# Tokens and features on 512-byte addresses, the direct tiles moved behind three products, and two products exchanged

## The chip, the cores and the metric

The kernel runs on one core of one Trainium2 chip. The metric is device time in microseconds (us) of one execution. The kernel before took 2361.76 us, the median of three runs (2360.01 to 2362.44).

## The reference, cut to what matters

One layer of a streaming encoder over 2048 prompt tokens and 128 sample tokens (8 sequences of 16), model width 1024, float32 throughout:

```python
z = x @ w_in                       # 1024 -> 2824: q, k, v, output gate, 8 gate columns, attention q, k, v
hm = head_norm(mlstm(q, k, v, log gates)) * sigmoid(output gate)     # 4 heads x 128, in chunks
ha = sliding_window_attention(rope(qa), rope(ka), va, sinks)         # 8 query heads, 2 key heads
h = layer_norm(alpha * x + concat(hm, ha) @ w_out)
u = h @ w_up                       # 1024 -> 5632, value | gate
c = causal depthwise conv of width 3 over u
y = layer_norm(alpha * h + (silu(c_gate) * c_value) @ w_down)        # 2816 -> 1024
```

The outputs are y of both parts and the new states (mLSTM matrices, key and value rows, the last rows before the conv).

## The kernel before, in words

Every large product is made from float32 numbers split in two: `split` (lines 215 to 218) makes a high part by a cast to the type that TensorE takes (`scalar.copy`, ScalarE) and a low part by a subtraction (`vector.tensor_sub`, VectorE). A product is then three matmuls: high by high, high by low, low by high. One operand of a matmul is stationary (loaded into the array, 128 x 128), the other moves through it. The projections also use a seven-product scheme over 2 x 2 quadrants: products 1 to 7 take sums of quadrants of weights and of tokens.

There are four stages. The input projection (`i_dense`) runs over four token blocks (`IBLOCKS`); the sample tile, number 16, belongs to block 0. In a block it makes seven products for each of five groups `g` of 512 columns (`i_product`, L700), for block 0 also the sample tile's part (L710), and "direct" tiles (`i_direct`, L726): the remaining 264 columns (gates, key, value), one token tile at a time, without the seven-product scheme. Between them run small chains of the mLSTM and the attention. Then come the output projection (`group`, L222 to L224), the up projection (`f_product`, L1842) and the down projection (`f_downs`, L2045).

In groups 0 and 1 the weights are stationary and the tokens move; in groups 2 to 4 the tokens are stationary and the weights move. In the up projection the features move; in the output and down projection tokens or features are stationary.

The order of the matmuls is the order in which the program issues them. For the input projection it is the list `items`, made in `i_begin`: `("p", b, g, s)` is product s of group g in block b, `("t", b, i, e)` direct tile i of block b with the gate weights of edition e. `uq` lists the weight units in that order; `next_raw` issues a unit's load on SyncE's queue, `next_split` splits it, and `advance` does as many of both as there are free buffers (four raw slots `wraw`, eight halves). `x_load` loads token quadrants, `x_steps` makes their sums ("t1" to "t4") and splits, `x_single` those of the sample tile. VectorE and ScalarE take their work in an order that the framework chooses, SyncE's queue likewise.

At the start, block 0 has its direct tiles 2, 3 and 4 first, then products (g 0, s 1), (g 0, s 2), (g 1, s 1), (g 0, s 7), (g 0, s 6); its direct tiles 0 and 1 come at the end of the block, beside tiles 2 and 3 of block 1. Nine matmuls on zeros (`warm_up`, L325) stand ahead of all. Loads of the first quadrants are 512 KB each. After product (g 0, s 1) ScalarE copies its accumulator (bank A) to bank B (L775) before product 2 may go on in A.

Tiles lie in memory pools that are stacked by size, so a tile added to one pool moves all pools behind it. Before, the token halves (`oh`, `ol`) start 96 bytes past a multiple of 512 bytes in each partition, the features' halves 96 (products 2, 5, 3), 128 (product 4) or 480 bytes (products 1, 7, 6 and the down projection's `fu`) past one; the split weights lie at 192, 320, 448 and 64 past one, and two later slots (`wex`) at 96.

## Time and profile before

| what | value |
|---|---|
| median of the runs | 2361.76 us |
| time of the profiled execution | 2359.6 us |
| its span, first to last instruction | 2357.8 us |
| TensorE busy with matmuls | 2316.6 us, 98% of the span |
| VectorE busy | 1805.4 us, 77% |
| ScalarE busy | 1297.9 us, 55% |
| mean share of the DMA engines' time | 77.3% in the main queue |
| granted TensorE clock, mean | 0.997 |

PE is TensorE's matmul, PEld its weight load, which runs beside the matmul before it; DVE is VectorE, ACT ScalarE, POOL GpSimd, SPq the queue of transfers on SyncE. A matmul's recorded duration includes the time in the pipe, so matmuls overlap in the records; what a matmul costs is the busy time of a stretch divided by the number of matmuls in it. A `<-` names what a tile is made from, `x36` a count, and the bracket at the end of a row of the timeline the idle time before it and what ended that.

### The profile page before, as it was taken

The page shows a single profiled execution, that of the slowest core. Times are in us where ns is not written, and L with a number is a line of the kernel's source. Part 1 is how long each engine was busy: PE and PEld are TensorE (multiplying, and loading weights), DVE is VectorE, ACT ScalarE, POOL GpSimd, SP SyncE. Part 2 cuts the span into 40 slices and gives each one's busy share as a digit, 9 for nine tenths or more (in the row PEclk, how much of TensorE's full clock was granted, in tenths as well). Part 3 has the DMA queues.
Part 4 walks back from the last instruction along what each step waited for, and adds up shares of the span by engine and source line. Part 5 has one row for each costly group of instructions (what it writes and reads, how often), then busy time and mean ns, then how long its engine had stood idle before and what let it go on. Part 6 is the DMA issues. An engine that isn't in the chain of part 4 may idle for free.

```text
span 2357.8 us, 39882 instructions
## 1 busy us (share of the span) xinstructions
PE 2316.6 (98%) x14425; PEld 2123.4 (90%) x14425; DVE 1805.4 (77%) x3150; ACT 1297.9 (55%) x2465; POOL 243.4 (10%) x298
## 2 busy tenths in 40 slices
PE   8999999999999999999999999999999999999998
PEld 7999998999987777999999999999999978888876
DVE  8677586796678888987788677768766776795897
ACT  5353466676666664655556555555554544554643
POOL 0101101101212221300001000002100100000100
PEclk9999999999999999999999999999999999999999
DMA  7788899889977657787777989887988786757653
GB/s 278 263 308 291 282 290 313 285 289 319 301 259 247 210 208 251 264 324 277 281 270 252 309 314 318 303 271 263 321 286 265 230 283 203 240 186 226 233 181 108
DMA packets 296933, 624.98 MB, mean 265 GB/s; under 512 B 47004, under 2 KB 140192, under 8 KB 296736
## 3 DMA queue, kind: packets, MB, share of 16 engines
q1 hardware_dynamic: 295872, 619.29, 77.3%
q10 hardware_dynamic: 864, 3.15, 0.4%
q8 instruction: 114, 1.87, 0.3%
q14 instruction: 83, 0.68, 0.1%
HBM read 451.78 MB, written 170.56 MB: 264 GB/s over the span
## 4 chain that ended last, share of the span: by engine, by line
PE 73%; DVE 5%; DMA 2%; issue 2%; ACT 2%; POOL 0%; SPq 0%; DVEq 0%; ACTq 0%; POOLq 0%
PE dps L1842 18%; PE fup L1842 18%; PE dps L700 7%; PE dps L2045 7%; PE fht L2045 6%; PE fup L2045 6%; PE dps L222 2%; PE dps L224 2%; PE dps L223 2%; PE ppo L1337 1%; PE psc L1288 1%; PE ppt L1331 1%; PE dps L726 1%; DVE w L218 1%; DVE hl L218 1%
## 5 line engine op out<-in xcount | busy, mean ns | idle before, releaser
L1842 PE MATMUL dps<-hh,uw 128*128 128x384 f32 (+1 forms) x1848 | 481.0, 329 | 6.7 <-ACT u L1867 1.9
L1842 PE MATMUL fup<-hh,uw 128*128 128x384 f32 (+1 forms) x1848 | 479.8, 328 | 2.7 <-ACT u L1867 2.6
L1842 PEld LDWEIGHTS dps<-hh,uw 128*128 128x128 f32 x1848 | 330.0, 188 | 10.5 <-ACT u L1867 2.7
L1890 DVE SCALAR_TENSOR_TENSOR cc<-u,cw,cc 128x768 f32<-128x768 f32 (+1 forms) x264 | 252.4, 977 | 107.5 <-ACT cc L1888 105.5
L1842 PEld LDWEIGHTS fup<-hh,uw 128*128 128x128 f32 x1848 | 330.1, 188 | 4.0 <-ACT u L1867 3.5
L1842 PE MATMUL fup<-hl,uw 128*128 128x384 f32 (+1 forms) x924 | 302.8, 328 | 1.6 <-DVE hl L218 1.6
L1842 PE MATMUL dps<-hl,uw 128*128 128x384 f32 (+1 forms) x924 | 302.4, 327 | 0.0
L700 PE MATMUL dps<-w,oh 128*128 128x256 f32 x1344 | 259.3, 286 | 2.8 <-ACT zev L759 1.0
L218 DVE TENSOR_TENSOR w<-wraw,w 128x1024 fp32r<-128x1024 f32 (+2 forms) x167 | 190.4, 1148 | 58.8 <-ACT w L217 58.1
L217 ACT CAST w<-wraw 128x1024 fp32r<-128x1024 f32 (+2 forms) x167 | 163.0, 985 | 129.1 <-PE dps L700 52.9
L217 ACT CAST uw<-wraw 128x1024 fp32r<-128x1024 f32 x126 | 122.9, 978 | 189.3 <-PE dps L2045 108.8
L700 PEld LDWEIGHTS dps<-w,oh 128*128 128x128 f32 x1344 | 213.1, 189 | 14.7 <-issue 8.9
L1888 ACT ACTIVATE cc<-u,cw 128x768 f32<-128x768 f32 (+1 forms) x132 | 129.6, 998 | 123.0 <-DVE u L1881 61.4
L218 DVE TENSOR_TENSOR uw<-wraw,uw 128x1024 fp32r<-128x1024 f32 x126 | 142.4, 1132 | 71.0 <-ACT uw L217 70.2
L700 PE MATMUL dps<-w,ol 128*128 128x256 f32 x672 | 189.6, 282 | 0.0
L700 PE MATMUL dps<-oh,w 128*128 128x256 f32 x896 | 171.1, 285 | 8.2 <-ACT dps L775 2.9
L1842 PEld LDWEIGHTS fup<-hl,uw 128*128 128x128 f32 x924 | 173.6, 188 | 2.5 <-DVE hl L218 2.5
L2045 PE MATMUL fup<-uw,fu 128*128 128x512 f32 x726 | 174.1, 396 | 1.6 <-DVE uw L218 1.6
L1842 PEld LDWEIGHTS dps<-hl,uw 128*128 128x128 f32 x924 | 173.6, 188 | 0.0
L2045 PEld LDWEIGHTS fup<-uw,fu 128*128 128x128 f32 x726 | 136.3, 188 | 34.9 <-DVE uw L218 2.1
L2045 PE MATMUL dps<-uw,fu 128*128 128x512 f32 x660 | 165.0, 396 | 0.0
L700 PEld LDWEIGHTS dps<-oh,w 128*128 128x128 f32 x896 | 140.9, 188 | 14.7 <-issue 4.1
(331 smaller groups left out, 4624.7 us busy)
## 6 DMA issues: line engine op xcount, KB each, us to landing
uw<-zw SPq DMA_DIRECT2D x176, 512.0 KB, 4.9
zw<-uw SPq DMA_DIRECT2D x88, 512.0 KB, 2.9
w<-zws SPq DMA_DIRECT2D x72, 512.0 KB, 6.6
wv<-wup SPq DMA_DIRECT2D x66, 512.0 KB, 5.5
wraw<-wi SPq DMA_DIRECT2D x65, 512.0 KB, 4.9
wraw<-zt SPq DMA_DIRECT2D x60, 512.0 KB, 4.1
wraw<-wdn SPq DMA_DIRECT2D x45, 512.0 KB, 3.7
wraw<-wo SPq DMA_DIRECT2D x40, 512.0 KB, 4.5
```

The costliest lines, as they stand in the source:

```text
L217: nc.scalar.copy(hi, src)
L218: nc.vector.tensor_sub(lo, src, hi.bitcast(F32))
L222: mm(out, ah, bh, start=start, stop=False)
L223: mm(out, ah, bl, start=False, stop=False)
L224: mm(out, al, bh, start=False, stop=stop)
L700: mm(o, l, r, start=s in (1, 7) and c == k == i == 0, stop=k == 3 and i == 2, skip_group_check=True)
L726: mm(o, x, w, start=k == i == 0, stop=k == KD - 1 and i == 2, skip_group_check=True)
L1288: nc.tensor.matmul(ps[kvh][:, j, :nk], q[rs, j0 + j], k[rs, sel], start=i == 0, stop=i == 2)
L1842: mm(ps, l[:, k], r[:, k], start=s in (1, 7) and k == 0 and i == 0, stop=k == 3 and i == 2, skip_group_check=True)
L1888: S.activation(c[:, v], u[:, v, 2:2 + n], AF.Identity, bias=w[3], scale=w[2])
L1890: V.scalar_tensor_tensor(c[:, v], u[:, v, i:i + n], w[i], c[:, v], op0=ALU.mult, op1=ALU.add)
L2045: mm(ps, l[:, k, c], r[:, k], start=s in (1, 4, 7) and u == 0 and k == 0 and i == 0, stop=u == nu - 1 and k == n - 1 and i == 2, skip_grou ...
```

## The change

Three things are changed together.

First, positions. `skew(pool, n)` adds an unused tile of n bytes to a pool. With four of them, and the small tile `nst` moved from the pool of weights to a later one, the token halves, all halves of features and `fu` start on multiples of 512 bytes; the split weights stay where they were, at 64, 192, 320 and 448 past one, and the two later slots come to 64.

Second, the start. The products (g 0, s 1), (g 0, s 2), (g 1, s 1) come first, then all five direct tiles of block 0, then products 7 and 6. The end of block 0 has no direct tiles of its own any more. The first weight and token quadrants are loaded and split in parts, the first product takes its matmuls in the order in which the parts come, the gate weights are loaded into free token slots instead of the four raw slots, sums of weights for product 6 are made behind the split for product 7, and the steps that make token quadrants are issued between the products (`begin`) instead of all ahead.

Third, order within a product. Where tokens are stationary (groups 2 to 4, and the sample tile's part), each three matmuls go high by high, low weight by high token, high weight by low token; before, the last two were the other way round.

```diff
+    def skew(self, pool, n):
+        pool.tile([P, n // 4], F32, name="skew", tag=f"skew{n}", bufs=1)
+
     def split(self, hi, lo, src):
...
             wx, wxcm = enter("wx1sb")
+            self.skew(wx, 64)
             self.unit_more(wx)
...
             self.wx, wxcm = enter("wx2sb")
+            self.skew(self.wx, 64)
             self.f2, f2cm = enter("f2sb")
...
             self.f_ups(n)
+            self.skew(self.f2, 480)
+            self.skew(self.wx, 448)
             close(f3cm)
...
             if b == 0:
-                it += [("t", 0, i, -1) for i in (2, 3, 4)]
-                it += [("p", 0, 0, s) for s in (1, 2)] + [("p", 0, 1, 1)] + [("p", 0, 0, s) for s in (7, 6)]
+                it += [("p", 0, 0, s) for s in (1, 2)] + [("p", 0, 1, 1)]
+                it += [("t", 0, i, -1) for i in (0, 1, 2, 3, 4)] + [("p", 0, 0, s) for s in (7, 6)]
             else:
...
                     it += [("p", b, g, s) for s in (6, 7, 5, 2, 3, 4)]
-            it += [("t", b, i, b) for i in (0, 1)]
+            if b:
+                it += [("t", b, i, b) for i in (0, 1)]
             if b + 1 < nb:
...
         there = u[0] == "p" and u[1] == 0 and (u[2] == 0 and u[3] != 1 or u[3] in (5, 4, 3) or u[2:] == (1, 1))
+        there = there or u[:2] == ("g", -1)
         if not there and not self.kept(u) and not self.raw_free():
...
         elif u[0] == "g":
-            self.raw_of[u] = e = self.raw_slot([P, 2, 264])
+            if u[1] < 0:
+                e = [self.xp.tile([P, 2, 264], F32, name="graw", tag=("oh5", "ol5", "oh6", "ol6")[u[2]], bufs=1), False]
+            else:
+                e = self.raw_slot([P, 2, 264])
+            self.raw_of[u] = e
             nc.sync.dma_start(e[0], a["wg"][u[2]])
...
                 nc.sync.dma_start(self.zws[g][SUMS.index(m)][0], r[q])
-        if s == 7:
-            V.tensor_sub(r[a11], r[a11], r[a21])
-            keep(a11, 7)
-        elif s == 6:
+        def sums():
             V.tensor_add(r[a21], r[a21], r[a22])
...
             keep(a11, 6)
+        if s == 7:
+            V.tensor_sub(r[a11], r[a11], r[a21])
+            keep(a11, 7)
+        elif s == 6 and g:
+            sums()
         q = {1: a11, 7: a11, 6: a11, 2: a12, 3: a12, 5: a21, 4: a22}[s]
...
                 nc.sync.dma_start(self.zws[g][SUMS.index(s)][i].rearrange("p a b -> p (a b)"), t.bitcast(F32))
+        if s == 7 and g == 0:
+            sums()
         if s == (6 if g == 0 else 2):
...
                 self.hx[b, s] = h, l = self.x_slot(4 if s == "b12" else s)
-                n = 4 if (b, s) == (0, "b12") else 1
+                n = 4 if (b, s) == (0, 1) else 1
                 for i in range(n):
...
             self.raw_of[0, q] = self.raw_slot([P, 4, HT])
-        for q in ((0, 0), (0, 1), (1, 0), (1, 1)):
-            self.nc.sync.dma_start(self.raw_of[0, q][0], self.a["wi"][0][q])
...
+        def quad(*q):
+            nc.sync.dma_start(self.raw_of[0, q][0], a["wi"][0][q])
+
         self.next_raw()
-        self.x_load(0, 2)
-        for _ in range(3):
-            self.next_raw()
-        self.x_load(0, 4)
+        first, x1 = self.raw_of[0, (0, 0)][0], self.x_raw(1)
+        self.xr[0, 1] = x1
+        for k in (slice(0, 2), slice(2, 4)):
+            nc.sync.dma_start(first[:, k], a["wi"][0][0, 0][:, k])
+            nc.sync.dma_start(x1[:, k], a["xq"][0][0, 0][:, k])
         self.single_raw = self.tp.tile([P, KD, P], F32, name="xsr", tag="pth", bufs=2)
-        nc.sync.dma_start(self.single_raw, a["xs"])
+        nc.sync.dma_start(self.single_raw[:, :4], a["xs"][:, :4])
+        quad(0, 1)
+        self.x_load(0, 3)
+        nc.sync.dma_start(self.single_raw[:, 4:], a["xs"][:, 4:])
+        for q in (2, 4):
+            for _ in range(2 + (q == 2) * 2):
+                self.next_raw()
+            self.x_load(0, q)
+        quad(1, 0)
+        quad(1, 1)
         self.angles = {}
+        self.rope_load(IBLOCKS[0][0], 2)
         self.rope_load(IBLOCKS[0][2], 2)
...
         self.next_split()
-        self.x_steps(0, "b12")
-        for _ in range(3):
-            self.next_split()
-        self.x_steps(0, 3)
-        self.x_single(1, 2)
-        self.x_load(0, 1)
-        self.next_raw()
-        self.x_load(0, 3)
         self.x_steps(0, 1)
-        self.advance()
-        self.x_steps(0, 2, "t3", 7, "t2", 6)
-        self.x_single(4)
-        self.x_steps(0, "t1", 5, "t4")
+        self.x_single(1)
+        self.next_split()
+        self.x_steps(0, 2)
+        self.x_single(2)
+        self.next_split()
+        begin = {("p", 0, 0, 1): ["b12"], ("p", 0, 0, 2): [3], ("p", 0, 1, 1): ["t3", 7],
+                 ("t", 0, 0, -1): ["t2", 6], ("t", 0, 2, -1): ["t1", 5, "t4"]}
         self.sb, self.trans = {}, None
...
                     self.gates[b] = self.tp.tile([P, 5, 8], F32, name="gates", tag="gates", bufs=2)
-                ps = self.bank([P, 512], "pg") if ti == 4 else self.ib[ti % 2 * 2]
+                ps = self.bank([P, 512], "pg") if ti == 4 or e < 0 and ti % 2 == 0 else self.ib[ti % 2 * 2]
                 yield from self.i_direct(b, ti, e, ps)
                 self.i_keys(b, ti, ps)
-                if ti == 1:
+                if ti == 1 and b:
                     if b + 1 < nb:
...
                     self.release(4)
+                elif item in begin:
+                    self.x_steps(0, *begin[item])
+                if ti == 3 and b or ti == 4:
                     self.x_steps(b, 4)
...
                 self.t_setup()
-            if (g, s) == (1, 6):
+            if b and (g, s) == (1, 6):
                 self.rope_load(IBLOCKS[b][0], 2)
...
                         self.x_steps(b + 1, x)
+            if (b, g, s) == (0, last, 4):
+                self.x_steps(1, 1, 2)
+                after = [6, 1]
             if g == last and b + 1 == nb and s in (7, 5, 2, 3):
...
                 self.advance()
+                self.x_steps(0, *begin.get(item, ()))
+                if item == ("p", 0, 0, 2):
+                    self.x_single(4)
...
         hh, hl = self.hx[b, s]
-        for c in range(2):
+        pairs = [(0, 0), (1, 0), (0, 2), (1, 2)] if (b, g, s) == (0, 0, 1) else [(0, 0), (0, 2), (1, 0), (1, 2)]
+        for c, k0 in pairs:
             m = slice(c * P, c * P + P)
             o = ps[:, c * HT:(c + 1) * HT]
-            for k in range(4):
-                for i, (w, x) in enumerate(((wh, hh), (wh, hl), (wl, hh))):
+            for k in (k0, k0 + 1):
+                for i in range(3):
+                    w, x = ((wh, hh), (wh, hl), (wl, hh))[i if g < 2 else (0, 2, 1)[i]]
                     l, r = (w[:, k, m], x[:, k]) if g < 2 else (x[:, k, m], w[:, k])
                     mm(o, l, r, start=s in (1, 7) and c == k == i == 0, stop=k == 3 and i == 2, skip_group_check=True)
-                if k % 2:
-                    yield 645
+            yield 645
         if b == 0 and s in (1, 2, 5, 4):
...
             for k in range(4):
-                for i, (w, x) in enumerate(((wh, xh), (wh, xl), (wl, xh))):
+                for i, (w, x) in enumerate(((wh, xh), (wl, xh), (wh, xl))):
                     mm(o, x[:, k], w[:, k], start=s == 1 and k == i == 0, stop=s in (2, 4) and k == 3 and i == 2, skip_group_check=True)
...
         V, S = nc.vector, nc.scalar
-        one = lambda n, w: self.wp.tile([P, w], F32, name=n, tag=n, bufs=3)
+        one = lambda n, w: self.f2.tile([P, w], F32, name=n, tag=n, bufs=3)
         s = one("nst", 4)
...
             ln2.append(t)
+        self.skew(self.fp, 480)
         self.in_down = True
...
```

## The prediction

> **What bounds the kernel now.** I read the page's first two parts, then the stretches by stage, then the chain and the timeline of the first 62 us.
>
> ```profile
> PE 2316.6 (98%) x14425; PEld 2123.4 (90%) x14425; DVE 1805.4 (77%) x3150; ACT 1297.9 (55%) x2465; POOL 243.4 (10%) x298
> PE   8999999999999999999999999999999999999998
> DVE  8677586796678888987788677768766776795897
> PE dps L1842 18%; PE fup L1842 18%; PE dps L700 7%; PE dps L2045 7%; PE fht L2045 6%; PE fup L2045 6%; PE dps L222 2%; PE dps L224 2%; PE dps L223 2%; PE ppo L1337 1%; PE psc L1288 1%; PE ppt L1331 1%; PE dps L726 1%; DVE w L218 1%; DVE hl L218 1%
> ```
>
> The matmul stream is the bound nearly everywhere: PE is below nine tenths in the first and the last slice alone, and the chain is matmuls line after line. So two things can move the time: what one matmul costs in the stream, and the holes, which lie at the start. For the first, the stretches in which one line runs alone (columns: stretch, its us, PE busy and count, PEld busy and count, clock, DMA share, GB/s):
>
> ```profile
> 60.00:245.00 185.00, 136.48 (x1116) 1.00 0.84 287
> 1290.00:1590.00 300.00, 298.07 (x1695) 294.75 (x1694) 1.00 0.88 303
> 1700.00:1870.00 170.00, 170.00 (x1160) 169.75 (x1159) 1.00 0.87 276
> 1940.00:2280.00 340.00, 340.00 (x1459) 273.69 (x1458) 1.00 0.65 214
> ```
>
> Busy time by count: 122.3 ns for the 256 columns of L700 (ends of products included), 175.9 ns for 384 columns of L1842, 146.6 ns for its 320 columns in the last block, 233.0 ns for 512 columns of L2045. That is 0.455 to 0.458 ns a column for the last three: the stream runs at one pace, with no hole to speak of. For the second, the start:
>
> ```profile
> 1.97 4.21 PE L325 MATMUL dps<-zero 128*128 128x512 f32 x9 [1.97 <-DVE zero L320]
> 5.98 0.56 PE L726 MATMUL dps<-w,oh 128*128 128x264 f32 x1
> 10.63 0.81 PE L726 MATMUL dps<-w,oh 128*128 128x264 f32 x2 [1.45 <-ACT oh L562]
> 18.54 3.07 PE L726 MATMUL pg<-w,xs 128*128 128x264 f32 x24
> 21.45 0.28 PE L700 MATMUL dps<-oh,w 128*128 128x256 f32 x1
> 28.70 0.38 PE L700 MATMUL dps<-oh,w 128*128 128x256 f32 x1 [2.87 <-ACT dps L775]
> 31.66 1.59 PE L710 MATMUL psx<-w,xs 128*128 128x256 f32 x12
> 7.06:10.48 3.42, 1.68 (x11) 1.26 (x10) 2.59 (x5) 2.58 (x4) 0.00 (x0) 1.00 1.01 399
> 10.48:17.30 6.82, 6.21 (x26) 5.91 (x27) 5.45 (x10) 4.04 (x11) 0.00 (x0) 0.50 1.03 415
> 21.45:41.50 20.05, 15.86 (x132) 15.45 (x131) 20.05 (x25) 11.39 (x14) 0.00 (x0) 1.00 0.62 208
> PE dps L700 <- DVE w L218: 1.3, 1, 1.3
> ```
>
> The first real matmul is at 5.98, behind the nine on zeros. Three direct tiles then take until 21.45, 15.5 us, though a tile at full pace takes 2.93 (24 matmuls at 0.122, from the row at 18.54, whose last 0.15 us is the pipe): 8.8 for three, 6.7 lost. Half of that loss is the clock: after a stretch of 3.42 us in which PE was busy for 1.68 it was granted 0.50 for 6.82 us, which costs 3.4. The other half is waiting for tokens and gate weights. Then 2.9 us are lost at 28.70, where ScalarE's copy of a bank came late behind casts, and 1.3 for a weight's low part. From 5.98 until product (g 0, s 6) is through I count 11 us lost (6.7 + 2.9 + 1.3). From 21.45 to 41.50 VectorE (third pair of numbers) is busy for all of the 20.05 us: it sets the pace of the start as much as PE does.
>
> **The change part by part.**
>
> *The start.* Nothing is removed: the same matmuls run, the two direct tiles of block 0 (2 x 2.93 = 5.9 us of PE) are moved from the block's end to the start. What changes is what waits. The transfers, by the queue's rate in the first 45 us (40 slices of 1.125 us):
>
> ```profile
> GB/s 0 55 299 370 269 295 381 426 386 415 422 419 415 411 408 408 379 113 15 0 0 0 277 325 119 173 3 150 295 401 175 52 301 259 411 415 408 346 222 382
> 0.74 0.39 SPq L534 DMA_DIRECT2D xr<-xq  x1
> 4.61 0.41 ACT L562 CAST oh<-xr 128x256 fp32r<-128x256 f32 x1 [2.60 <-DMA xr<-xq]
> 14.82 1.06 ACT L562 CAST oh<-xr 128x1024 fp32r<-128x1024 f32 x1
> 14.90 0.23 DVE L864 TENSOR_TENSOR rb<-zev,ropet 128x64 f32<-128x64 f32 x1 [1.13 <-ACT zev L734]
> 15.62 0.29 DVE L867 TENSOR_TENSOR zev<-zev,rb 128x128 f32<-128x128 f32 x1
> 15.92 1.23 DVE L563 TENSOR_TENSOR ol<-xr,oh 128x1024 fp32r<-128x1024 f32 x1
> 440.80 4.96 PE dps L700 x42
> zws<-wraw SPq DMA_DIRECT2D x4, 512.0 KB, 3.8
> ```
>
> Summed up, 0.52 MB are there at 3.8 us, 1.05 at 5.3, 2.36 at 9.0, 3.15 at 11, 5.28 at 16. The changed order needs 1.05 MB for product 1 (weights and tokens), 2.36 until product 2's tokens, 3.15 until product (g 1, s 1), 5.28 until the last direct tile's tokens; with 0.8 from there to the first instruction (the first 0.52 MB were cast at 4.61), 1.06 for a cast and 1.23 for a subtraction these are ready at about 7 (in parts, the first near 5.2), 12, 14 and 19. PE starts at 6.0 as before, since the nine matmuls on zeros still stand ahead; product 1 with the sample's part is 36 matmuls at 0.118 (the row of 42), 4.25 us, of which the sample's twelve are 1.42, plus 0.5 for the clock that is still low until 7.06. At 10.8 it waits about 1.2 us for product 2's low tokens; after that the three products end at 20 and five direct tiles at 34.8 without a wait for transfers. The copy that came 2.9 us late is now followed, not led, by the next casts (they are issued behind it), so I cost it at 0.4, hidden beside the sample's twelve matmuls; were that cover gone, it is back to 2.9. Sum of what PE loses: 0.5 + 1.2 + 0.5 for the sample's split = 2.2 instead of 11.
>
> VectorE is what is late next. Ahead of product 7 it has about 30 us of work (20 subtractions and sums of 1.23 or their like in parts, five rope steps of four instructions, 1.0 each), ahead of product 6 another 4; started at 4.4 with 2.5 of waiting it reaches product 6 at about 41, PE at 38.5. So 2.5 of the 8.8 are given back: 6 to 9 saved, I take 7.
>
> *The end of block 0.* Before, two direct tiles (5.9 us) covered the split of block 1's first quadrant; now tile 2 of block 1 follows product 4 at once, and the slot it needs is freed by that product. Cast and subtraction, 2.3 us, less the sample's twelve matmuls, 1.4, that still stand between: 0.9 lost, 0 if the framework puts them first, 2.3 if last. The splits of quadrants 1 and 3 now run beside two tiles as they did. The queues: SyncE issues three more transfers at the start (0.4 us each, beside 5 us of PE on zeros), and the store of product 7's weights must have left before the sums for product 6 overwrite them (3.8 us, within 14.65 us of direct tiles). That sum waits on VectorE's queue, and splits that stand behind it there wait too; PE needs none of them before 35, so the wait is part of the 2.5 above.
>
> *Exchange where tokens are stationary.* The same matmuls and loads. The weight's low part is needed one matmul (0.12 us) sooner, the token's later. L726 and L2045 already have that order, and cost 0.122 for 264 columns and 0.233 for 512, the same per column as L700 and L1842: I take 0, ends -1 and +2 (the rows of waits show one such wait).
>
> *Positions.* No instruction is added. The question is whether a matmul's pace depends on where its operands lie. Rows of the chain show that it does, a little:
>
> ```profile
> 963.57 6.47 PE dps L1842 x36
> 1249.95 6.36 PE fup L1842 x36
> 1550.76 6.24 PE fup L1842 x36
> 1699.87 5.38 PE dps L1842 x36
> 1712.46 5.29 PE fup L1842 x36
> 1988.59 2.79 PE fht L2045 x12
> L1842 PE MATMUL dps<-hh,uw 128*128 128x384 f32 (+1 forms) x1848 | 481.0, 329 | 6.7 <-ACT u L1867 1.9
> L1842 PE MATMUL dps<-hl,uw 128*128 128x384 f32 (+1 forms) x924 | 302.4, 327 | 0.0
> ```
>
> Three products of the same shape take 6.24 to 6.47 us, 173.3 to 179.7 ns a matmul, with no wait between. But no feature or token tile lies on a multiple of 512 in this trace, and those at 96, 128 and 480 past one show the same spread, so nothing says that 512 is the good place. Bounds: L1842 has 5544 matmuls (both banks), two thirds, 3696, at 384 columns, 1848 at 320. All at the fastest row: 2.5 x 3696 = -9.4, and 0.5 x 2046 = -1.1 in the down projection (2.79 / 12 = 232.5; 2046 matmuls by the program): -10.5. All at the slowest: 3.9 x 3696 = +14.2 and 2.9 x 1848 = +5.3 (5.38 / 36 = 149.4): +19.5. Between them I take 0: the weights keep four positions out of which all the present spread comes, and the mean of the stretches is nearer the fast end already. Loads to aligned tiles may land sooner; no load is what PE waits for after 62 us.
>
> The sum against the profiled execution: 2359.6 - 7 + 1 + 0 + 0 = 2353.6. It ran 2.2 under the median shown, so 2355.8 in medians: 2356.
>
> **The rivals.**
>
> *The pace improves.* What speaks for it is the spread above and that tokens and features are now all in one phase against the weights; against it, that three phases show no difference. At the fast rows everywhere: 2356 - 10.5 = 2345. The Trainium skill, TensorE: Matmul & The Clock Gate, section "Wait — 56ns, not 53.3ns?", gives 215.7 ns for 512 columns of another type; the row here is 233.0, so they differ, and if position were the whole of that 17 ns the gain would by an estimate from that page be above 100 us, which I hold unlikely.
>
> *The pace gets worse*, the rival on the other side. [...] 2356 + 19.5 = 2375. It decides as soon as the 11,800 matmuls of L700, L1842, L222 to L224 and L2045 cost 0.5 ns more each, 6 us, which eats the start.
>
> *The start gives nothing.* PE's wait ahead of product 2 is one more hole at 10.8, and the clock drops again: the trace shows 0.50 after a stretch half busy. That is 3.4 us, and with VectorE late by 2.5 more at product 6 nothing is left: 2361. The Trainium skill, the same page, section "What's actually happening", has the clock fall after an idle window of about 3.4 us; by that rule a wait of 1.2 us would leave it up and this rival falls, but the trace does not agree, since it fell after a stretch with 1.68 of 3.42 us busy.
>
> **How the numbers follow.** The forecast, 2356, has 0.36, with its own range 2349 to 2361 (the start 4 to 9 either way of its bounds, positions -5 to +4). The better pace 0.25, the worse 0.22, the start without gain 0.17. A difference under 0.2%, 4.7 us, can't be told from none in this kernel: faster is below 2357, slower above 2366.5. Faster: three quarters of the forecast and the better pace, 0.52. Same: a quarter of it and 0.13 of the last, 0.22. Slower: the worse pace and the rest, 0.26. The range for 8 in 10 cuts a tenth on either side: 2338, below 2345 since the fast rows bound only what this trace shows, to 2373.
>
> **What would show it.** The start: the five direct tiles end near 35, no half clock after 7.06, and product 6 is through at 42 to 44 with 5.9 us more done than before. The block's end: a wait of about 1 us in front of L726 near 245. Positions: the four stretches again, 122, 176, 147, 233 ns if I am right; a shift of 1 ns in them is worth 12 us, more than all the rest, and is what would make the prediction wrong. The exchange: L700's groups 2 to 4 at the same busy time by count.

## The result and the profile after

The changed kernel takes 2348.28 us, the kernel before, measured beside it, 2361.07: a ratio of 0.9947, with a 95% interval of 0.9934 to 0.9961. Of its four runs (2346.93, 2347.46, 2349.09 and 2812.64 us) the last was slow, at a granted clock of 0.752 where the others had 0.997 to 0.998, and the ratio leaves it out. The profiled execution has a span of 2345.7 us, 12.1 less than the 2357.8 before. The first lines of the page, and its chain of the end:

```profile
span 2345.7 us, 39856 instructions
PE 2303.0 (98%) x14425; PEld 2116.3 (90%) x14425; DVE 1803.9 (77%) x3150; ACT 1298.1 (55%) x2465; POOL 243.8 (10%) x298
PE   9999999999999999999999999999999999999998
PE dps L1876 18%; PE fup L1876 18%; PE dps L735 12%; PE dps L2080 6%; PE fup L2080 6%; PE fht L2080 6%; PE dps L225 2%; PE dps L227 2%; PE dps L226 2%; PE dps L760 2%; DVE w L221 1%; DMA txy<-wdn 1%; PE ppo L1371 1%; PE psc L1322 1%; PE ppt L1365 1%
```

Lines have moved: L700, L710, L726, L1842 and L2045 of before are now L735, L744, L760, L1876 and L2080; the split is L220 and L221. The matmuls are as many as before, 14425, and TensorE's busy time is 13.6 us less. So the matmuls themselves cost less; holes that were closed would not show in it.

Where along the span the time went is read from the timeline, by the first matmuls of the stages (columns: start, duration, engine, line). Before: the product (g 0, s 1) of block 1, the up projection, the down projection, and the last matmuls:

```profile
170.51 0.28 PE L700 MATMUL dps<-oh,w 128*128 128x256 f32 x1
941.20 0.42 PE L1842 MATMUL fup<-hh,uw 128*128 128x384 f32 x1
1885.64 1.64 PE L2045 MATMUL fup<-uw,fu 128*128 128x512 f32 x6
2346.73 3.43 PE L2045 MATMUL fht<-uw,fu 128*128 128x512 f32 x14
```

The same four of the changed kernel:

```profile
166.33 0.28 PE L735 MATMUL dps<-oh,w 128*128 128x256 f32 x1
934.25 0.42 PE L1876 MATMUL fup<-hh,uw 128*128 128x384 f32 x1
1878.72 1.63 PE L2080 MATMUL fup<-uw,fu 128*128 128x512 f32 x6
2334.69 3.40 PE L2080 MATMUL fht<-uw,fu 128*128 128x512 f32 x14
```

Block 0 is 4.2 us shorter, the rest of the input projection with the output projection 2.8, the up projection the same (944.44 and 944.47), the down projection 5.1. More than half lies after block 0, where the program changed in positions and in the order of two of the three matmuls only.

The pace shows it. Stretches in which one line's matmuls are counted (columns: stretch, its us, PE busy and count, clock, DMA share, GB/s); first tokens moving in block 1, before:

```profile
172.00:200.00 28.00, 25.63 (x216) 1.00 0.92 321
```

and of the changed kernel the same place, 384 and 320 columns of the up projection (with the weight load's busy time beside), and the down projection:

```profile
168.00:196.00 28.00, 25.62 (x223) 1.00 0.90 318
1290.00:1590.00 300.00, 298.08 (x1698) 294.71 (x1697) 1.00 0.87 302
1700.00:1870.00 170.00, 169.42 (x1155) 169.09 (x1154) 1.00 0.85 268
1940.00:2270.00 330.00, 330.00 (x1433) 1.00 0.66 216
```

Busy time by count: 118.7 ns went to 114.9 for 256 columns with tokens moving, 233.0 to 230.3 for 512 columns of the down projection. 384 columns (175.8 and 175.6) and 320 (146.6 and 146.7) stayed. The table below has finer means, from one matmul's start to the next one's.

The start, from the timeline: the first product's matmuls, the sample's twelve, product 2's first, the sample's of the third product, the first and the last rows of direct tiles, and product 5's first. Below them, with all engines (PE, PEld, DVE, ACT, POOL, then clock, DMA share, GB/s), the stretch after 7 us and the one with a low clock:

```profile
5.98 0.41 PE L735 MATMUL dps<-oh,w 128*128 128x256 f32 x1
9.32 1.57 PE L744 MATMUL psx<-w,xs 128*128 128x256 f32 x12
12.70 0.39 PE L735 MATMUL dps<-oh,w 128*128 128x256 f32 x1 [1.80 <-ACT dps L809]
17.29 1.60 PE L744 MATMUL psx<-w,xs 128*128 128x256 f32 x12
22.98 0.40 PE L760 MATMUL pg<-w,oh 128*128 128x264 f32 x2
36.23 1.50 PE L760 MATMUL pg<-w,xs 128*128 128x264 f32 x11
43.86 0.39 PE L735 MATMUL dps<-oh,w 128*128 128x256 f32 x1 [0.69 <-ACT zev L801]
7.00:10.42 3.42, 3.42 (x30) 3.42 (x31) 1.45 (x3) 2.00 (x4) 0.00 (x0) 1.00 1.01 369
13.53:16.94 3.41, 3.41 (x19) 3.41 (x18) 3.41 (x5) 1.78 (x4) 0.00 (x0) 0.50 1.04 416
```

Three products end at 23.0 and five direct tiles at 37.6, where the next product starts. Product 2 waited 1.8 us, and behind that hole the clock was 0.50 for 3.41 us. What ScalarE and VectorE did in the hole:

```profile
10.60 1.04 ACT L579 CAST oh<-xr 128x1024 fp32r<-128x1024 f32 x1 [0.20 <-DMA xr<-xq]
11.55 0.61 ACT L591 CAST xs<-xsr 128x512 fp32r<-128x512 f32 x1
12.07 0.58 ACT L809 COPY dps<-dps 128x512 f32<-128x512 f32 x1
11.67 1.23 DVE L580 TENSOR_TENSOR ol<-xr,oh 128x1024 fp32r<-128x1024 f32 x1
```

The copy of the bank (L809, the old L775) stood behind casts, and the low tokens (`ol`) of product 2 were ready at 12.90 only. The end of block 0 has a new wait:

```profile
158.29 0.41 PE L760 MATMUL dps<-w,oh 128*128 128x264 f32 x2
160.63 0.39 PE L760 MATMUL dps<-w,ol 128*128 128x264 f32 x1 [1.93 <-DVE ol L580]
```

### The profile page after: what moved, and what is told of

Read it like the earlier page. It is cut to its first block, busy times and chain, and to the rows that moved or that the text cites. A ratio compares the mean times of both kernels' runs of the same rounds, so it can differ in the third digit from the quotient of the medians.

```text
span 2345.7 us, 39856 instructions
## 1 busy us (share of the span) xinstructions
PE 2303.0 (98%) x14425; PEld 2116.3 (90%) x14425; DVE 1803.9 (77%) x3150; ACT 1298.1 (55%) x2465; POOL 243.8 (10%) x298
## 4 chain that ended last, share of the span: by engine, by line
PE 81%; DVE 8%; DMA 6%; issue 2%; ACT 2%; POOL 1%; SPq 0%; DVEq 0%; ACTq 0%; POOLq 0%
PE dps L1876 18%; PE fup L1876 18%; PE dps L735 12%; PE dps L2080 6%; PE fup L2080 6%; PE fht L2080 6%; PE dps L225 2%; PE dps L227 2%; PE dps L226 2%; PE dps L760 2%; DVE w L221 1%; DMA txy<-wdn 1%; PE ppo L1371 1%; PE psc L1322 1%; PE ppt L1365 1%
## 5 line engine op out<-in xcount | busy, mean ns | idle before, releaser
L1876 PE MATMUL dps<-hh,uw 128*128 128x384 f32 (+1 forms) x1848 | 480.8, 328 | 7.5 <-ACT u L1901 2.4
L1876 PE MATMUL fup<-hh,uw 128*128 128x384 f32 (+1 forms) x1848 | 478.9, 328 | 2.9 <-ACT u L1901 1.8
L1876 PEld LDWEIGHTS dps<-hh,uw 128*128 128x128 f32 x1848 | 329.8, 188 | 11.6 <-ACT u L1901 3.8
L1876 PEld LDWEIGHTS fup<-hh,uw 128*128 128x128 f32 x1848 | 329.8, 188 | 3.9 <-ACT u L1901 2.4
L1876 PE MATMUL fup<-hl,uw 128*128 128x384 f32 (+1 forms) x924 | 302.4, 327 | 1.8 <-DVE hl L221 1.8
L1876 PE MATMUL dps<-hl,uw 128*128 128x384 f32 (+1 forms) x924 | 302.1, 327 | 0.0
L735 PE MATMUL dps<-w,oh 128*128 128x256 f32 x1344 | 249.2, 286 | 7.3 <-ACT zev L801 3.7
L221 DVE TENSOR_TENSOR w<-wraw,w 128x1024 fp32r<-128x1024 f32 (+2 forms) x163 | 189.5, 1169 | 52.8 <-ACT w L220 52.0
L220 ACT CAST uw<-wraw 128x1024 fp32r<-128x1024 f32 x126 | 122.8, 977 | 184.6 <-PE dps L2080 106.4
L735 PEld LDWEIGHTS dps<-w,oh 128*128 128x128 f32 x1344 | 206.2, 189 | 20.5 <-issue 10.0
L220 ACT CAST w<-wraw 128x1024 fp32r<-128x1024 f32 (+2 forms) x163 | 160.9, 993 | 91.5 <-PE dps L735 40.5
L221 DVE TENSOR_TENSOR uw<-wraw,uw 128x1024 fp32r<-128x1024 f32 x126 | 142.4, 1131 | 67.4 <-ACT uw L220 66.8
L735 PE MATMUL dps<-w,ol 128*128 128x256 f32 x672 | 188.4, 280 | 0.0
L1876 PEld LDWEIGHTS fup<-hl,uw 128*128 128x128 f32 x924 | 173.4, 188 | 2.5 <-DVE hl L221 2.5
L735 PE MATMUL dps<-oh,w 128*128 128x256 f32 x896 | 169.4, 285 | 6.3 <-ACT zev L793 2.6
L2080 PE MATMUL fup<-uw,fu 128*128 128x512 f32 x726 | 172.1, 393 | 1.7 <-DVE uw L221 1.7
L1876 PEld LDWEIGHTS dps<-hl,uw 128*128 128x128 f32 x924 | 173.4, 188 | 0.0
L2080 PEld LDWEIGHTS fup<-uw,fu 128*128 128x128 f32 x726 | 136.2, 188 | 33.1 <-DVE uw L221 2.2
L2080 PE MATMUL dps<-uw,fu 128*128 128x512 f32 x660 | 163.2, 393 | 0.0
L735 PEld LDWEIGHTS dps<-oh,w 128*128 128x128 f32 x896 | 141.7, 191 | 12.5 <-issue 4.1
```

What stands on the lines that cost most here:

```text
L220: nc.scalar.copy(hi, src)
L221: nc.vector.tensor_sub(lo, src, hi.bitcast(F32))
L735: mm(o, l, r, start=s in (1, 7) and c == k == i == 0, stop=k == 3 and i == 2, skip_group_check=True)
L1876: mm(ps, l[:, k], r[:, k], start=s in (1, 7) and k == 0 and i == 0, stop=k == 3 and i == 2, skip_group_check=True)
L2080: mm(ps, l[:, k, c], r[:, k], start=s in (1, 4, 7) and u == 0 and k == 0 and i == 0, stop=u == nu - 1 and k == n - 1 and i == 2, skip_grou ...
```

## The experiments

Every ratio is to the kernel before on the same chip; it is formed from all counted runs of both and so is not quite the quotient of the medians beside it. Runs of one kernel scatter more than I had assumed: the eleven of the kernel with the start alone lie between 2353.67 and 2363.23 us. So the profiled execution of a kernel can stand some us off its median, and the reasons rest on rows as much as on ratios.

### One part alone

**Positions alone, on the kernel before:**

```diff
+            self.skew(wx, 64)
...
+            self.skew(self.wx, 64)
...
+            self.skew(self.f2, 480)
+            self.skew(self.wx, 448)
...
-        one = lambda n, w: self.wp.tile([P, w], F32, name=n, tag=n, bufs=3)
+        one = lambda n, w: self.f2.tile([P, w], F32, name=n, tag=n, bufs=3)
...
+        self.skew(self.fp, 480)
```

> The kernel before with the positions alone. By the theory that the gain is the pace of the matmuls: the first matmul of the up projection (941.2 before, 934.2 after) comes 6 to 8 us earlier, the down projection is 5 us shorter, the up projection unchanged, and the whole takes 2346 to 2350, at least as little as the changed kernel. By the rival that the start carries the gain and positions do nothing: 2361, with 233 ns a matmul in the down projection as before.

**The new start alone** (the changed kernel with the lines above taken out and the old order of the three matmuls):

> The changed kernel with the positions and the exchange taken back, so the new start alone. If the start is worth what was forecast: -6, 2355. By the theory that it wins 7 us up to product (g 0, s 6) and gives 4 or more back at the end of block 0, where the first direct tile of block 1 waits for its low tokens: -2 to -3, 2358 to 2359, with the wait of about 2 us near 160 in the trace. Pace of all stages as before: 118 ns for 256 columns, 233 for 512.

**The changed kernel without the exchange:**

```diff
-                for i in range(3):
-                    w, x = ((wh, hh), (wh, hl), (wl, hh))[i if g < 2 else (0, 2, 1)[i]]
+                for i, (w, x) in enumerate(((wh, hh), (wh, hl), (wl, hh))):
...
-                for i, (w, x) in enumerate(((wh, xh), (wl, xh), (wh, xl))):
+                for i, (w, x) in enumerate(((wh, xh), (wh, xl), (wl, xh))):
```

> The changed kernel with the exchange alone taken back. If it is worth nothing, as forecast: 2348, within 1 us of the changed kernel, and groups 2 to 4 at 117 ns a matmul. By the rival that the two stationary tiles in a row which are now the same bring the 1.3 ns that L735 gains in these groups: 2.7 us more, 2351.

| kernel | median, us | before, us | ratio |
|---|---|---|---|
| positions alone | 2349.32 | 2362.57 | 0.9951 [0.9939, 0.9964] |
| start alone | 2359.38 | 2362.57 | 0.9987 [0.9978, 0.9996] |
| all but the exchange | 2347.49 | 2362.57 | 0.9941 [0.9928, 0.9954] |

Positions alone give what the whole change gives; the start alone gives 3 us; the exchange gives nothing that can be told. Whether the start's 3 us come on top of the positions these ratios don't settle: 0.9951 times 0.9987 is 0.9938, and the two kernels that have both measured 0.9947 and 0.9941, the changed kernel a second time 0.9966 (below). With the positions alone and the old start, block 1 begins as early as in the changed kernel. Its rows, product (g 0, s 1) of block 0 and of block 1:

```profile
18.48 0.28 PE L707 MATMUL dps<-oh,w 128*128 128x256 f32 x1
166.28 0.28 PE L707 MATMUL dps<-oh,w 128*128 128x256 f32 x1
```

The first explains part of the second: 18.48 stands where the kernel before has 21.45, though nothing was changed in that part but addresses. The 6.82 us at half clock of the kernel before (10.48 to 17.30) were no part of this execution; it had 3.4 us, at 26, where TensorE was busy anyway. So the clock has to be set apart. The table gives for each profiled execution the start of block 1 and of the up projection, the us at half clock up to there (from the clock of all stretches of 1 us), and both starts less half of it, which is what half clock costs where TensorE has work, and too much where it waits.

| kernel | block 1 | half clock | less half | up projection | half clock | less half |
|---|---|---|---|---|---|---|
| before | 170.5 | 6.8 | 167.1 | 941.2 | 10.2 | 936.1 |
| changed | 166.3 | 3.4 | 164.6 | 934.3 | 10.2 | 929.1 |
| positions alone | 166.3 | 3.4 | 164.6 | 932.7 | 10.2 | 927.6 |
| start alone | 167.7 | 6.8 | 164.3 | 936.3 | 10.3 | 931.2 |

In these executions, one of each kernel, each part alone gets block 0 2.5 to 2.8 us shorter, and both together no more. Up to the up projection the half clock is the same in all four, so the start saved nothing there by the clock: what it avoided at 10 us came later.

### Is it the multiple of 512?

After the first runs two readings were open: that tokens and features gain by lying on multiples of 512 bytes, or that the distance between the stationary and the moving operand counts. The next four move them apart.

**Tokens and features 64 bytes past a multiple of 512, weights where they were:**

```diff
+            self.skew(self.wp, 64)
...
-        self.skew(self.fp, 480)
+        self.skew(self.fp, 416)
```

> The changed kernel with tokens and features 64 bytes past a multiple of 512, the split weights where they were. If it is the multiple of 512 that counts: the pace of before comes back, 118 ns for 256 columns with tokens moving and 233 for 512 in the down projection, 2358. If any common phase on 64 bytes does it: 114.6 and 230.6 as in the changed kernel, 2348.

**Everything 64 bytes further**, so that tokens, features and weights keep their distances:

```diff
+            self.skew(self.cp, 64)
...
-        self.skew(self.fp, 480)
+        self.skew(self.fp, 416)
```

> The changed kernel with everything, weights too, 64 bytes further, so that the distance from tokens to weights stays and the multiple of 512 is given up. If the distance between what moves and what is loaded counts: 2348 and 230.6 ns in the down projection. If the multiple of 512 counts by itself: 2358 and 233.

**Tokens and features 256 past a multiple of 512:**

```diff
+            self.skew(self.wp, 256)
...
-        self.skew(self.fp, 480)
+        self.skew(self.fp, 224)
```

> The changed kernel with tokens and features 256 bytes past a multiple of 512, the weights where they were: the set of distances to the weights is the same, the multiple is one of 256 only. If 256 suffices, or the distance counts: 2348. If it must be 512: 2358, at 118 and 233 ns.

**Tokens and features on multiples of 512, weights 32 bytes further** (96, 224, 352, 480), which restores the distances that tokens and weights had before, at other addresses:

```diff
+            self.skew(self.cp, 32)
...
-            self.skew(wx, 64)
+            self.skew(wx, 96)
...
-            self.skew(self.wx, 64)
+            self.skew(self.wx, 96)
...
-            self.skew(self.wx, 448)
+            self.skew(self.wx, 416)
...
+            self.skew(self.wp, 32)
...
-        st = self.wp.tile([P, 2, 6], F32, name="st", tag="st", bufs=1)
+        st = self.f2.tile([P, 2, 6], F32, name="st", tag="st", bufs=1)
```

> The changed kernel with tokens and features on multiples of 512 as they are and the split weights 32 bytes further, so that the distance is an odd multiple of 32 again, as before the change. By the theory that only the distance counts: the gain in pace is gone, 118 ns for 256 columns with tokens moving, 233 in the down projection, 2358. By the rival that tokens and features on multiples of 512 are what counts: 114.6 and 230.6, 2348.

The ratios, with ns from one matmul's start to the next one's (means over consecutive records; "T" tokens moving, groups 0 and 1; "W" weights moving, groups 2 to 4), and how far, in bytes, the starts of stationary and moving tile lie from a multiple of 128 of each other, without sign, in the token products:

| kernel | distance | ratio | 256 T | 256 W | 384 | 320 | 512 down |
|---|---|---|---|---|---|---|---|
| before | 32 | 1 | 117.9 | 118.5 | 174.4 | 146.6 | 233.3 |
| start alone | 32 | 0.9987 | 117.9 | 118.5 | 174.4 | 146.6 | 233.3 |
| weights 32 further | 32 | 1.0010 [1.0000, 1.0019] | 118.0 | 118.5 | 174.6 | 146.6 | 233.4 |
| changed | 64 | 0.9947 | 114.6 | 117.2 | 174.2 | 146.6 | 230.7 |
| positions alone | 64 | 0.9951 | 114.8 | 117.0 | 174.2 | 146.6 | 230.7 |
| all 64 further | 64 | 0.9956 [0.9939, 0.9973] | 114.7 | 117.1 | 174.1 | 146.6 | 230.6 |
| tokens at 256 | 64 | 0.9957 [0.9941, 0.9972] | 114.9 | 117.1 | 174.1 | 146.5 | 230.7 |
| tokens at 64 | 0 | 0.9983 [0.9973, 0.9993] | 119.0 | 118.7 | 175.2 | 146.6 | 230.6 |

(The medians of the last four experiments in the order told: 2355.03, 2348.57 and 2350.11 beside 2359.99; 2362.15 beside 2360.36.) The multiple of 512 has nothing to do with it: with everything 64 further and with tokens at 256, the weights 64 away in both, the gain stays, and tokens on multiples of 512 with the weights 32 away lose all of it, to within 0.2 ns of the kernel before in every column. (This kernel has the new start too, and at 1.0010 it is slower than the start alone, 0.9987. Its profiled execution has 10.3 us of waits between block 1 and the up projection against 7.2, and 20.5 us at half clock up to there against 10.3; why is open.) The rows behind it: tokens moving in block 1, then the down projection; first with the weights 32 further,

```profile
172.00:200.00 28.00, 25.63 (x215) 1.00 0.89 307
1940.00:2270.00 330.00, 330.00 (x1415) 1.00 0.65 213
```

then with everything 64 further,

```profile
172.00:200.00 28.00, 25.63 (x223) 1.00 0.86 299
1940.00:2270.00 330.00, 330.00 (x1432) 1.00 0.65 217
```

and with tokens at 64, where the token products lose their gain (25.62 / 214 = 119.7 ns) and the down projection keeps it (330 / 1433 = 230.3), although four fifths of its matmuls lie at distance 0 there too; for them 0 is no worse than 64:

```profile
168.00:196.00 28.00, 25.62 (x214) 1.00 0.89 300
1940.00:2270.00 330.00, 330.00 (x1433) 1.00 0.65 216
```

The distance folded to 128 is still a mixture. The addresses of the built programs, set against the matmuls of the traces in order, give every matmul its own distance, moving tile minus stationary tile. Taken modulo 256 (first column), it sorts the ns from start to start; where several of the seven kernels (before, start alone, changed and the four of this section) have a distance, the range of their means is given:

| distance | 256 T | 256 W | 384 | 512 down |
|---|---|---|---|---|
| 0 | 119.3 | 118.5 | 173.6 to 173.8 | 229.8 |
| 32 | 117.1 to 117.4 | | 174.6 to 175.7 | |
| 64 | 114.7 to 115.0 | 117.8 to 117.9 | 173.4 to 173.5 | 229.4 to 230.1 |
| 96 | | 119.0 | | 233.8 to 234.1 |
| 128 | 118.5 | 119.0 | 176.0 | 231.5 to 232.7 |
| 160 | 118.4 to 118.6 | | 173.9 to 174.0 | |
| 192 | 114.2 to 114.6 | 116.4 to 116.5 | 174.6 to 176.4 | 232.5 |
| 224 | | 117.9 to 118.0 | | 232.8 |

(The 384 columns still differ by 1 to 2 ns between kernels at 32 and at 192.) So the changed kernel has not the best of it: its four weight slots lie at 64 and at 192 modulo 256, and the down projection's matmuls take 229.4 ns on one pair of slots and 232.5 on the other. A kernel with every slot at 64 was not run.

Why a distance costs some ns is not shown: no run here looks at how the array's operands are read.

### The end of block 0

**Direct tile 1 back at the end of block 0**, as cover for the split of block 1's tokens:

```diff
-                it += [("t", 0, i, -1) for i in (0, 1, 2, 3, 4)] + [("p", 0, 0, s) for s in (7, 6)]
+                it += [("t", 0, i, -1) for i in (0, 2, 3, 4)] + [("p", 0, 0, s) for s in (7, 6)]
...
-            if b:
-                it += [("t", b, i, b) for i in (0, 1)]
+            it += [("t", b, i, b) for i in (0, 1) if b or i]
...
-            if (b, g, s) == (0, last, 4):
-                self.x_steps(1, 1, 2)
-                after = [6, 1]
```

> The changed kernel with direct tile 1 of block 0 put back to the end of the block, so that it covers the split of block 1's first quadrant; tile 0 stays at the start. If that wait (1.9 us near 158) is what the start gives back: 2346, 2 us less, and no wait of that kind in the trace. By the rival that the work in front of it is late for VectorE anyway: the wait turns up at the tile after it or at product 7 of the start, and the time is unchanged.

It measured 2350.48 beside 2362.57, 0.9953 [0.9939, 0.9967], beside 0.9941 for the kernel without the exchange on the same chip: no better. The wait for the low tokens is gone, but a wait of 1.0 us for another tile of VectorE (`zev`) stands in its place, and product 5, now at 39.72 instead of 43.86, comes earlier to work of VectorE and ScalarE. Behind its first matmul up to block 1 the waits are 7.0 us, in the changed kernel 6.4. A hole in its timeline, with the stretch that follows (PE, clock, DMA share, GB/s):

```profile
57.98 0.39 PE L731 MATMUL dps<-oh,w 128*128 128x256 f32 x1 [2.02 <-ACT dps L825]
58.80:62.20 3.40, 3.40 (x19) 0.50 0.92 310
```

Block 1 starts at 167.72, later than the changed kernel's 166.33. The cover that is put back at the block's end is taken from the start, and by the sum of the waits it hid as much there.

**The split of block 1's tokens one product earlier**, into a slot that is free by then, so that the low tokens come sooner and no tile has to cover them. It was measured twice, the second time beside the changed kernel itself:

```diff
-                self.hx[b, s] = h, l = self.x_slot(4 if s == "b12" else s)
+                self.hx[b, s] = h, l = self.x_slot((5 if b == 1 else 4) if s == "b12" else s)
...
-        passages = [{1: ["load"], 7: ["t3", 7], 6: ["t2", 6], 3: [3, "t4"], 4: ["b12", "t1"]},
+        passages = [{1: ["load"], 7: ["t3", 7], 6: ["t2", 6], 3: ["b12", 3, "t4"], 4: ["t1"]},
```

> The changed kernel with block 1's first quadrant for direct tiles split one product sooner, into a slot that product 5 has left, so that product 4 of block 0 covers it. If the wait of 1.9 us near 158 is what the block's end costs: it is gone from the trace and the time is 2 us less, 2346. By the rival that VectorE is behind as a whole there: the wait turns up within the next product and the time stays at 2348.

> The changed kernel itself, beside the next one on the same chip: 0.9947 of the time before, as measured first.

> The kernel with the early split of block 1's first quadrant once more. If it saves the 1.9 us wait: 0.9939, 2 us under the changed kernel in the same call. If the wait only moves: 0.9947. What half clock there is in a single execution may hide either, so the medians decide.

The first time it took 2344.82 us beside 2360.36, 0.9944 [0.9928, 0.9959]; the second 2346.45 beside 2359.51, 0.9939 [0.9925, 0.9952], with the changed kernel beside it on that chip at 2351.40, 0.9966 [0.9955, 0.9978]. In the second run's timeline the low part follows the high one without a wait, and block 1 starts at 163.26:

```profile
157.42 0.41 PE L760 MATMUL dps<-w,oh 128*128 128x264 f32 x2
157.67 0.28 PE L760 MATMUL dps<-w,ol 128*128 128x264 f32 x1
163.26 0.28 PE L735 MATMUL dps<-oh,w 128*128 128x256 f32 x1
```

Less half of the half clock up to there, block 1 starts at 163.3 and 163.4 in its two executions, 164.6 and 164.9 in the two of the changed kernel: 1.2 to 1.6 us gained of the 1.9 that the wait had. This version beats the kernel before clearly and, on the one chip where both ran, the changed kernel too; how much of that 0.27% is the wait and how much the scatter of half clock and waits is open, since the rows account for less than 2 us of it. Against the changed kernel's first measurement, 0.9947, its 0.9944 and 0.9939 are no difference that can be told.

## Why the direction of the prediction held and its terms did not

I forecast 2356 us with an own range of 2349 to 2361; 2348.28 lies below it and nearest the rival of a better pace, 2345, to which I gave 0.25. "Faster" came true, for another reason than the one that I thought likeliest: the forecast rested on the start, 6 us, which gave 3 alone, and took positions at nothing, which gave 13. That the direction held was luck as far as the likeliest case goes. The sign that I had named for being wrong, a shift of the stretches' pace, is what came.

- *Positions, 0.* The step that failed is the sentence "those at 96, 128 and 480 past one show the same spread, so nothing says that 512 is the good place". I sorted the rows by where tokens and features lie, and the cause is where they lie against the weights. By that measure (the second table above) the trace of before held 32, 96, 160 and 224 for L700 and 96, 128 and 224 for the down projection: the good distances, 64 and 192 for the one and 64 for the other, were not among these, and its fast rows could not bound the gain. So the term that I took at 0 was 13 us. The bounds show it: -1.1 us for the down projection, which gained 5.1; none at all for L700, whose spacing fell by 1.3 to 3.3 ns; and -9.4 for the up projection, which gained nothing. That "three phases show no difference" was wrong too: in the trace of before the 384 columns took 173.4 ns at a distance of 64 and 176.0 at 128. But the change moved the features from one set of distances to another with nearly the same mean, 174.4 and 174.2. And the output projection had the gain in sight: its 162 matmuls of 816 that read weights from the two later slots, at distance 0, took 229.7 ns, the others 232.6 and 233.7.
- *The start up to product 6.* Forecast 7 us saved; on the trace product 5 starts at 43.86 instead of 45.47 with 5.9 us more of direct tiles done, 7.5. But 1.7 of it is the clock (3.4 us at half clock up to there instead of 6.8), and the clock did not go as said: the stretch from 7.00 to 10.42 was full and at 1.00, as forecast, and the half clock came at 13.53, behind the hole before product 2. Three products ended at 23.0 instead of 20. Product 2 waited 1.8 where I had 1.2. I had the copy followed by the next casts; it stood behind them, at 12.07, and the trace ends the wait with it. But the low tokens, on which my 1.2 rested, came at 12.90 instead of 12, and the second matmul of product 2 started at 12.95, so without the copy most of the hole would have stayed. In my sum, 8.8 less 2.5 is 6.3, not 7.
- *VectorE late, 2.5 given back before product 6.* Nothing of the kind before product 6; it comes after it. The waits of the changed kernel from behind product 5's first matmul to block 1, then the same of the kernel before:

```profile
PE dps L760 <- DVE ol L580: 1.9, 1, 1.9
PE dps L735 <- ACT zev L801: 1.7, 1, 1.7
PE dps L735 <- DVE zev L805: 1.1, 1, 1.1
PE dps L735 <- DVE zev L807: 0.9, 1, 0.9
PE dps L735 <- ACT dps L829: 0.8, 1, 0.8
```

```profile
PE dps L700 <- DVE zev L773: 1.0, 1, 1.0
PE dps L700 <- DVE zev L771: 0.7, 1, 0.7
PE dps L700 <- ACT zev L767: 0.6, 1, 0.6
```

  6.4 us instead of 2.3: 4.1 given back inside block 0. These rows fit that TensorE came earlier to chains on VectorE and ScalarE that did not come earlier; no run moved those chains alone.
- *The end of block 0, +1 (0.9 wait).* The wait is where it was forecast (I wrote near 245; it is at 158) and what it was forecast to be, the low tokens of block 1's first quadrant; it measured 1.9. The term was too small by half.
- *The exchange, 0.* Right: 0.9941 without it, 0.9947 with it.
- *The rivals.* "The start gives nothing" described the start better than the forecast did: by the medians it is worth 3 us alone, and beside the positions nothing that can be told. Its mechanism, a hole before product 2 and a clock drop behind it, is what the timeline shows at 12.70 and 13.53. The rule that was weighed there (the Trainium skill, TensorE: Matmul & The Clock Gate, section "What's actually happening": half speed after an idle window of about 3.4 us), taken as a window without matmuls, fails here too: the 3.41 us ahead of the drop were busy for 1.60 (PE, clock, DMA share, GB/s of the changed kernel):

```profile
10.12:13.53 3.41, 1.60 (x13) 1.00 1.02 398
```

  "The pace gets worse" had the sign wrong for this change; tokens at 64, with 119.0 ns for 256 columns with tokens moving and 175.2 for 384, shows its case in small.

Summed up by spacing and counts: 1344 matmuls of 256 columns with tokens moving at 3.3 ns, 2016 with weights moving at 1.3, the output projection's 816 at 1.6 (232.7 before, 231.1 after) and the down projection's 1980 of 512 columns at 2.65 make 4.4 + 2.6 + 1.3 + 5.2 = 13.5 us, an estimate from the counts of the changed kernel's groups and the table. The down projection, whose 1980 matmuls I had counted as 2046, gave its share in full, 5.1. From block 1 to the up projection the shortening was 2.8, or 4.5 without the clock, less than the spacings promise there; the waits of that stretch add up to 9.7 us, before to 8.3, which is a part of the rest.

## What to carry to other kernels

When the array is busy for 98% of the span, look at the spacing of its matmuls before the holes: 1 to 3 ns of 115 to 233 were worth four times what a reordered start gave. Sort the spacings by the relation of the two operands' addresses, not by either address alone, and keep in mind that rows of a trace bound only what varies in it: where a value of the relation does not occur, its effect is not zero but unknown, and one run with a few unused bytes tells it. Work that is moved ahead of a late engine can be given back in waits for that engine, as 4.1 us were here; issuing the split one product earlier took its wait out of the rows, where the one cover that was tried only moved waits.

## What the runs showed of the hardware that was not expected

The distance between stationary and moving tile, with its sizes in the two tables. For 256 columns with tokens moving: 114.6 ns where the starts lie 64 bytes off a multiple of 128 of each other, 117.9 at 32 and 119.0 at 0. For 512 columns of the down projection, modulo 256: 229.4 to 230.1 at 0 and 64, 231.5 to 234.1 at 96 to 224. For 320 columns: 146.5 to 146.6 in every kernel. Only these distances were run.

The low clock comes in steps of 3.4 us at different places in executions of the same program. The changed kernel had it at 13.5, 290 and 338 in one profile and at 10, 290, 338 and 914 in another, whose first and last such rows are (PE, clock, DMA share, GB/s)

```profile
9.95:13.30 3.35, 3.35 (x18) 0.50 1.05 417
914.50:917.70 3.20, 3.20 (x13) 0.50 0.90 305
```

and over all profiles up to the up projection it was between 6.8 and 20.5 us, which is up to 7 us of scatter. The Trainium skill, TensorE: Matmul & The Clock Gate, section "What's actually happening", says that the window of activity is free-running and does not start with the kernel; the shift between executions agrees with that. What the busy share does not show: at 290 the drop came after a stretch that counts as fully busy. The changed kernel, the stretch ahead, the drop, and a row of what ran ahead of it:

```profile
286.60:290.00 3.40, 3.40 (x29) 1.00 1.03 318
290.00:293.41 3.41, 3.41 (x17) 0.50 0.61 177
287.37 0.32 PE L1548 MATMUL ppo<-pts,vn 16*64 16x64 f32 x2
```

These are the attention's small matmuls, 64 columns wide, half of them on 16 rows. That it is their smallness that counts as idle is a guess; no run changed them.
